# One product of the next pass moved between the last two of a pass, and one quarter of y summed by accumulating DMA

## The chip, the cores and the metric

The kernel runs on one core of a Trainium2 chip, in one launch. The metric is device microseconds (us) of the whole program; three runs were taken, and the median counts. A profiled execution, from which all rows below come, is one further run.

The engines of the core are named as in the profile: PE (TensorE matmul; PEld is its weight load), DVE (VectorE), ACT (ScalarE), POOL (GpSimd) and SP (SyncE). Here POOL and SP mostly issue DMAs. Every engine works through its own list of instructions in order, so an instruction that waits holds up all behind it on that engine.

## The reference, cut to what matters

The layer is a norm, a joint projection, two kinds of attention, an output projection and an MLP with a squared ReLU. The change lies in the last product of the MLP and the sum around it, with 512 tokens, a model width of 2048 and a hidden width of 8192, all float32:

```python
def reference(x, ..., w_up, w_down, norm_final_g):
    ...
    x = x + mix @ w_out[layer]
    u = rmsnorm(x, norm_mlp_g[layer]) @ w_up[layer]
    x = x + jnp.square(jax.nn.relu(u)) @ w_down[layer]
    return rmsnorm(x, norm_final_g)
```

## The kernel before

**Precision.** Each float32 operand is split into a high part, a cast by ACT (`wh` of the weights, `uT` of the activations, line 94), and a low part, a subtraction by DVE (`wl` and the second half of `uT`, line 95). Each product is then three matmuls: high with high, high with low, low with high.

**The down phase** (lines 764 to 845) computes the product of the squared hidden layer with `w_down`. The hidden width is cut into 8 chunks `c` of 1024 rows and the 2048 output columns into 2 halves `n`; a pass is one pair (c, n), 16 in all. Within a pass the 2x2 block product is done by a scheme with 7 block products where 8 would be plain. Each takes sums of blocks of the activations (`o[0]` to `o[6]`, made once per chunk by `chunk_operands`) and sums of blocks of the weights (made in each pass by `down_weights`, a generator that yields the split pairs in the order in which they are used). A product is 24 matmuls of 128x512.

I call the seven products of a pass by the PSUM buffer into which they go: **U1** (`o[0]`), **V** (`o[1]`), **W1** (`o[2]`), **U2** (`o[3]`), **W2** (`o[4]`), **U3** (`o[5]`), **U4** (`o[6]`). Each buffer is two banks. V has its own buffer for each half and is summed over all chunks in PSUM. U1, U2, U3 and U4 add up in one buffer (`pU`) and W1, W2 in another (`pW`). After each of these the running sum is added into a quarter of `y` in SBUF by `to_y`, so U4, which adds to what U3 left, cannot start before `to_y` has read U3's sum. From pass to pass the buffers of U and W change places, since `if n: pU, pW = pW, pU`.

**Who sums y.** In chunks 1 to 6, `to_y` is a DVE add from PSUM (line 800) for W1, U2, W2, U3 and U4. For U1 it is an ACT copy into a tile `st` (line 797) and a DMA from POOL that adds `st` to y (line 798). In chunk 0 the first write of a quarter is an ACT copy into y; in chunk 7 all are DVE adds.

**Weights.** SP loads 512 KB tiles from HBM, and some sums of two blocks come from a second DMA that POOL issues and that adds to the tile in SBUF (line 681). The split pairs `wh`/`wl` have four buffers for the two pairs of each product, so the cast for a product two ahead waits until PE has read a pair of the present one.

The order on the engines is set by a scheduler that works with priorities. The weight work has a high one, and the activation work of the next chunk is pulled ahead into the pass before it. The first matmul of a product is kept in program order.

Of the kernel before, what the change touches and what calls it, by code (L numbers as in the profile page):

```python
# [9 lines left out]
F32 = mybir.dt.float32  # L10
F32R = mybir.dt.float32r
AF = mybir.ActivationFunctionType
ALU = mybir.AluOpType
AX = mybir.AxisListType

P = 128
# [3 lines left out]
NT = SEQ // P  # L20
# [15 lines left out]
def hymba_kernel(ctx: ExitStack, tc: tile.TileContext, x, x_t, norm_mix_g, w_dq, w_dk, w_dv, w_nq, w_nk, w_nv, lams,  # L36
                 subln_g, rel_bias, w_out, norm_mlp_g, w_up, w_down, norm_final_g, cos_t, sin_t, mask_t, out):
    nc = tc.nc
# [546 lines left out]
    for q in range(32):  # L585
# [3 lines left out]
        def prod(ps, s, first, last):  # L589
            th_, tl_ = next(ops)  # L590
            for k in range(8):
                for i, (a, j) in enumerate(((th_, 0), (th_, 1), (tl_, 0))):
                    nc.tensor.matmul(out=ps, lhsT=a[:, k], rhs=s[k // 4][:, j, k % 4], start=first and k + i == 0,  # L593
                                     stop=last and k == 7 and i == 2, skip_group_check=True)
# [26 lines left out]

    up_es.close()
    ps_up.close()
    psD = ctx.enter_context(tc.tile_pool(name="psD", bufs=2, space=bass.MemoryType.PSUM, reuse_waits="tile"))
    ypool = ctx.enter_context(tc.tile_pool(name="ypool", bufs=1, reuse_waits="tile"))
    wd2 = ctx.enter_context(tc.tile_pool(name="wd2", bufs=3, reuse_waits="tile"))
    y = ypool.tile([P, NT, DM], F32, name="y")
# [1 line left out]
    def chunk_operands(c):  # L629

        def load(m, th):
            t = rx.tile([P, 4, 256], F32, name="ur", tag="b")
            nc.sync.dma_start(out=t, in_=ud[4 * c:4 * c + 4, :, (2 * m + th) * 256:(2 * m + th + 1) * 256].rearrange(
                "j p t -> p j t"))
            return t

        pairs = []

        def part(src, neg=False):
            if not pairs or len(pairs[-1]) == 2:  # L640
                pairs.append([])
                pairs[-1].append(tpool.tile([P, 2, 2, 4, 256], F32R, name="uT", tag="T"))
                o = pairs[-1][0][:, 0]
            else:
                o = pairs[-1][0][:, 1]
                pairs[-1].append(None)
            if neg:
                nc.scalar.mul(o[:, 0], src, -1.0)
                nc.vector.scalar_tensor_tensor(out=o[:, 1], in0=src, scalar=-1.0, in1=o[:, 0].bitcast(F32),
                                               op0=ALU.mult, op1=ALU.subtract)  # L650
            else:
                split(o[:, 0], o[:, 1], src)
            return o

        with tc.high_priority(offset=700 if c else 250):
            u11, u12, u21, u22 = load(0, 0), load(1, 0), load(0, 1), load(1, 1)
            o = [part(u11), part(u12)]
            nc.vector.tensor_sub(out=u11, in0=u11, in1=u21)
            nc.vector.tensor_sub(out=u21, in0=u22, in1=u21)
            o.append(part(u21))  # L660
            f = rx.tile([P, 4, 256], F32, name="uf", tag="b")
            nc.vector.tensor_add(out=f, in0=u11, in1=u22)
            o.append(part(f, neg=True))
            nc.vector.tensor_sub(out=f, in0=f, in1=u12)
            o += [part(f), part(u11), part(u22)]
        return o
# [74 lines left out]
    def finish(t, lo, w, col):  # L741
        scaled(t, lo, w)
        squares(t, lo, w, col)
        times_g(t, lo, w)

    def norm_out(t, late=None, cols=3):

        ss = keep.tile([P, 1], F32, name="ssf", tag="ssf", bufs=2)
        nc.vector.tensor_reduce(out=ss, in_=ss3[:, t, :cols], axis=AX.X, op=ALU.add)
        r = rstd_of(keep, ss, DM, 1, "f")  # L750
        for i in ((0, 1, 2, 3) if late is None else (late, 0, 5 - late, 1)):
            qq = slice(i * 512, (i + 1) * 512)
            z = y[:, t, qq]
            if i == late:
                nc.vector.scalar_tensor_tensor(out=z, in0=z, scalar=r, in1=gF[1][:, (i - 2) * 512:(i - 1) * 512],
                                               op0=ALU.mult, op1=ALU.mult)
            elif i >= 2:
                nc.vector.tensor_scalar_mul(z, z, r)
            else:
                nc.scalar.mul(z, z, r)  # L760
            nc.sync.dma_start(out=out[t * P:(t + 1) * P, qq], in_=z)


    pVs = [None, None]
    n_down = [0]
    for c in range(8):
        o = chunk_operands(c)
        for n in range(2):
            end = c == 7 and n == 1
            ops = down_weights(c, n)  # L770
            pU, pW = (psD.tile([P, 2, 512], F32, name="pd", tag="pd") for _ in range(2))
            if n:
                pU, pW = pW, pU
            if c == 0:
                pVs[n] = psD.tile([P, 2, 512], F32, name="pv", tag="pv")
            pV = pVs[n]

            def prod(ps, s, w, first, last=True, blocks=(0, 1)):
                for u in range(2):
                    wh, wl = w[u]  # L780
                    for k in range(2):
                        for b in blocks:
                            sh, sl = (s[:, i, 2 * u + k, b * P:(b + 1) * P] for i in range(2))
                            for i, (l, r) in enumerate(((sh, wh), (sh, wl), (sl, wh))):
                                m = nc.tensor.matmul(out=ps[:, b], lhsT=l, rhs=r[:, k],  # L785
                                                     start=first and u + k + i == 0,
                                                     stop=last and u == 1 and k == 1 and i == 2, skip_group_check=True)
                                if u + k + i == 0:
                                    tc.keep_in_program_order(m)

            def to_y(ps, th, h, neg, fresh=False, dma=False):
                ys = y[:, 2 * th:2 * th + 2, n * 1024 + h * 512:n * 1024 + h * 512 + 512]
                if c == 0 and fresh:
                    nc.scalar.mul(ys, ps, -1.0 if neg else 1.0)
                elif dma:
                    st = wd2.tile([P, 2, 512], F32, name="st", tag="st", bufs=2)
                    nc.scalar.copy(out=st, in_=ps)
                    nc.gpsimd.dma_start(out=ys, in_=st, accum_op=ALU.add)
                else:
                    nc.vector.tensor_tensor(out=ys, in0=ys, in1=ps, op=ALU.subtract if neg else ALU.add)  # L800

            if end:
                for i in range(2):
                    gf = rx.tile([P, 1024], F32, name="gF", tag="b")
                    nc.sync.dma_start(out=gf, in_=norm_final_g[:, i * 1024:(i + 1) * 1024].broadcast_to([P, 1024]))
                    gF.append(gf)
                for t in range(NT):
                    finish(t, 0, 1024, 0)
            prod(pU, o[0], next(ops), True)
            to_y(pU, 0, 0, False, fresh=True, dma=c < 7)  # L810
            prod(pV, o[1], next(ops), c == 0, c == 7)
            if c == 7:
                to_y(pV, 0, 0, False)
            prod(pW, o[2], next(ops), True)
            to_y(pW, 1, 1, True, fresh=True)
            prod(pU, o[3], next(ops), False)
            to_y(pU, 0, 1, True, fresh=True)
            if end:
                for t in (0, 1):
                    finish(t, 1024, 512, 1)  # L820
            prod(pW, o[4], next(ops), False)
            to_y(pW, 0, 1, True)
            if end:
                for t in (0, 1):
                    finish(t, 1536, 512, 2)
                    norm_out(t)
            prod(pU, o[5], next(ops), False)
            to_y(pU, 1, 1, True)
            if not end:
                prod(pU, o[6], next(ops), False)  # L830
                to_y(pU, 1, 0, False, fresh=True)
                continue
            for t in (2, 3):
                finish(t, 1536, 512, 1)
                scaled(t, 1024, 512)
                nc.vector.tensor_add(out=ss3[:, t, 0:1], in0=ss3[:, t, 0:1], in1=ss3[:, t, 1:2])
            w4 = next(ops)
            for b in range(2):
                t = 2 + b
                prod(pU, o[6], w4, False, blocks=(b,))  # L840
                ys = y[:, t, 1024:1536]
                nc.vector.scalar_tensor_tensor(out=ys, in0=pU[:, b], scalar=qs[:, t:t + 1], in1=ys, op0=ALU.mult,
                                               op1=ALU.add)
                squares(t, 1024, 512, 1)
                norm_out(t, late=2, cols=2)


def _shape_tables():
# [82 lines left out]
```

## Time and profile before

| | |
|---|---|
| Median of 3 runs | 2166.03 us (2160.76 to 2166.07) |
| Profiled execution, its own time | 2166.34 us |
| Its span, first to last instruction | 2164.6 us |
| Mean granted TensorE clock | 0.988 of full speed |
| PE busy | 2091.2 us, 97% |
| DVE busy | 1550.5 us, 72% |
| ACT busy | 971.9 us, 45% |
| Down phase | from about 1484 us to the end of the span |

A busy share is an average over stages. PE's figure includes matmuls at a lower clock and the modelled ends of pipelined matmuls. The 1.7 us between the span and the execution's own time lie outside the first and last instruction.

### The profile page before, as it was taken

Reading aid. Unit: us, or ns where it says so; the run is one execution under the profiler, and the core shown is the slowest. Engines: PE = TensorE matmul, PEld = TensorE weight load, DVE = VectorE, ACT = ScalarE, POOL = GpSimd, SP = SyncE. Lnnn points to the kernel's source line nnn. Section 1 sums busy time; section 2 is a strip of 40 time slices with the busy share of each in tenths; the row PEclk is TensorE's granted clock in tenths of the full one; section 3 lists DMA queues with packets and bytes.
Section 4 is the critical chain, followed back from the end, with each engine's and each line's share of the span. In section 5 each row is a group of like instructions: output and inputs, shape, how many; then the busy total and the mean of one; then the engine's idle time right before and its main releaser. Section 6 shows DMA issues by size and latency. Waiting matters only on the chain.

```text
span 2164.6 us, 31127 instructions
## 1 busy us (share of the span) xinstructions
PE 2091.2 (97%) x12604; PEld 1860.7 (86%) x12604; DVE 1550.5 (72%) x1721; ACT 971.9 (45%) x1328; POOL 265.1 (12%) x257
## 2 busy tenths in 40 slices
PE   7999999999999999999999999999999999999986
PEld 6989989989888887999999999998777777777775
DVE  6656556556486437877777877788778778879788
ACT  4444444444354435444443444445544444444444
POOL 4221222122121000000000000000011110111100
PEclk8999999999999999999999999999999999999998
DMA  6332332332233741734334433447767767677663
GB/s 213 119 98 91 97 111 78 103 102 88 93 108 126 255 140 59 237 128 137 129 125 146 139 132 121 147 146 234 193 170 204 195 163 210 182 183 199 179 157 107
DMA packets 105745, 316.18 MB, mean 146 GB/s; under 512 B 11072, under 2 KB 27648, under 8 KB 105600
## 3 DMA queue, kind: packets, MB, share of 16 engines
q1 hardware_dynamic: 83040, 241.33, 33.4%
q0 software_dynamic: 22128, 72.31, 14.4%
q8 instruction: 99, 1.62, 0.3%
q10 hardware_dynamic: 432, 0.53, 0.1%
q14 instruction: 46, 0.38, 0.1%
HBM read 275.33 MB, written 30.25 MB: 141 GB/s over the span
## 4 chain that ended last, share of the span: by engine, by line
PE 85%; DVE 9%; issue 3%; ACT 1%; DMA 1%; SPq 0%; ACTq 0%; DVEq 0%
PE pm L593 27%; PE pd L785 17%; PE pa L141 8%; PE pa L98 7%; PE pa L99 7%; PE pa L100 7%; PE pv L785 4%; DVE wl L95 2%; DVE y L800 2%; PE pb L99 1%; PE pb L98 1%; PE pb L100 1%; PE pc L98 1%; PE pc L99 1%; PE pc L100 1%
## 5 line engine op out<-in xcount | busy, mean ns | idle before, releaser
L94 ACT CAST wh<-b 128x1024 fp32r<-128x1024 f32 x320 | 335.2, 1049 | 511.4 <-PE pd L785 255.6
L785 PE MATMUL pd<-wh,uT 128*128 128x512 f32 x1536 | 490.6, 397 | 36.4 <-DVE y L800 35.2
L95 DVE TENSOR_TENSOR wl<-b,wh 128x1024 fp32r<-128x1024 f32 x320 | 390.7, 1223 | 118.7 <-ACT wh L94 117.4
L785 PEld LDWEIGHTS pd<-wh,uT 128*128 128x128 f32 x1536 | 293.3, 191 | 107.8 <-ACT uT L94 22.0
L785 PE MATMUL pd<-wl,uT 128*128 128x512 f32 x768 | 305.0, 397 | 0.4 <-DVE wl L95 0.3
L593 PE MATMUL pm<-s,wh 128*128 128x256 f32 x1536 | 280.3, 284 | 3.4 <-ACT p L598 2.3
L593 PE MATMUL pm<-a,wh 128*128 128x256 f32 x1536 | 267.4, 279 | 2.0 <-DVE c L611 1.4
L593 PEld LDWEIGHTS pm<-s,wh 128*128 128x128 f32 x1536 | 239.6, 192 | 4.0 <-ACT p L598 2.8
L593 PEld LDWEIGHTS pm<-a,wh 128*128 128x128 f32 x1536 | 232.9, 189 | 2.4 <-DVE c L611 1.6
L95 DVE TENSOR_TENSOR wl<-ts,wh 128x1024 fp32r<-128x1024 f32 x128 | 154.9, 1223 | 105.1 <-ACT wh L94 103.5
L89 ACT CAST wh<-raw 128x1024 fp32r<-128x1024 f32 (+1 forms) x129 | 134.4, 1043 | 199.9 <-PE pa L99 72.1
L593 PE MATMUL pm<-s,wl 128*128 128x256 f32 x768 | 218.3, 284 | 1.5 <-DVE wl L95 1.5
L94 ACT CAST wh<-ts 128x1024 fp32r<-128x1024 f32 x128 | 132.6, 1051 | 186.3 <-PE pm L593 165.2
L141 PE MATMUL pa<-wh,hT 128*128 128x256 f32 x1024 | 201.4, 291 | 14.7 <-DVE hT L166 7.7
L593 PE MATMUL pm<-a,wl 128*128 128x256 f32 x768 | 209.8, 279 | 0.0
L90 DVE TENSOR_TENSOR wl<-raw,wh 128x1024 fp32r<-128x1024 f32 (+1 forms) x98 | 121.0, 1235 | 117.2 <-ACT wh L89 115.9
L100 PE MATMUL pa<-hT,wl 128*128 128x512 f32 x512 | 201.5, 394 | 0.0
L99 PE MATMUL pa<-hT,wh 128*128 128x512 f32 x512 | 201.1, 393 | 0.0
L98 PE MATMUL pa<-hT,wh 128*128 128x512 f32 x512 | 200.9, 392 | 0.0
L141 PEld LDWEIGHTS pa<-wh,hT 128*128 128x128 f32 x1024 | 168.4, 197 | 19.5 <-DVE hT L166 9.2
L785 PEld LDWEIGHTS pd<-wl,uT 128*128 128x128 f32 x768 | 146.9, 191 | 32.8 <-DVE wl L95 1.2
L593 PEld LDWEIGHTS pm<-s,wl 128*128 128x128 f32 x768 | 147.4, 192 | 1.9 <-DVE wl L95 1.9
(250 smaller groups left out, 3565.7 us busy)
## 6 DMA issues: line engine op xcount, KB each, us to landing
b<-in_w_down SPq DMA_DIRECT2D x130, 512.0 KB, 4.1
b<-in_w_up SPq DMA_DIRECT2D x128, 512.0 KB, 3.7
b<-in_w_down POOLq DMA_DIRECT2D x64, 512.0 KB, 9.1
raw<-in_w_out SPq DMA_DIRECT2D x32, 512.0 KB, 3.4
ud<-c POOLq DMA_DIRECT2D x32, 512.0 KB, 3.2
ur<-ud SPq DMA_DIRECT2D x32, 512.0 KB, 10.2
raw<-in_w_dq SPq DMA_DIRECT2D x16, 512.0 KB, 3.3
raw<-in_w_dk SPq DMA_DIRECT2D x16, 512.0 KB, 3.3
```

Of the source, the lines that this page charges most:

```text
L89: nc.scalar.copy(out=wh[:, cs], in_=raw[:, cs])
L90: eng.tensor_sub(out=wl[:, cs], in0=raw[:, cs], in1=wh[:, cs].bitcast(F32))
L94: nc.scalar.copy(out=hi, in_=src)
L95: (eng or nc.vector).tensor_sub(out=lo, in0=src, in1=hi.bitcast(F32))
L98: nc.tensor.matmul(out=ps, lhsT=lh, rhs=rh, start=first, stop=False)
L99: nc.tensor.matmul(out=ps, lhsT=lh, rhs=rl, start=False, stop=False)
L100: nc.tensor.matmul(out=ps, lhsT=ll, rhs=rh, start=False, stop=last)
L141: nc.tensor.matmul(out=ps[t], lhsT=a, rhs=b[:, k, :], start=first and i == 0, stop=last and i == 2, skip_group_check=True)
L593: nc.tensor.matmul(out=ps, lhsT=a[:, k], rhs=s[k // 4][:, j, k % 4], start=first and k + i == 0, stop=last and k == 7 and i == 2, skip_gro ...
L785: m = nc.tensor.matmul(out=ps[:, b], lhsT=l, rhs=r[:, k], start=first and u + k + i == 0, stop=last and u == 1 and k == 1 and i == 2, skip ...
L800: nc.vector.tensor_tensor(out=ys, in0=ys, in1=ps, op=ALU.subtract if neg else ALU.add)
```

## The change

Two buffers `X[0]` and `X[1]` (two banks each) take the place of the rotating `pU`/`pW`: pass p uses `X[p % 2]` as pU and the other as pW. The first product of pass p+1, with its weights and, at a new chunk, with its activation operands, is issued by `start_pass(p + 1)` between U3 and U4 of pass p. It goes into the buffer that was pW. The sum of the first quarter from U1 is now a DVE add. The quarter that W1 and U3 feed is now summed by ACT copies (with the sign) and accumulating DMAs from POOL in chunks 0 to 6, except for the first write of chunk 0.

```diff
-            prod(pU, o[0], next(ops), True)
-            to_y(pU, 0, 0, False, fresh=True, dma=c < 7)
...
-            prod(pW, o[2], next(ops), True)
-            to_y(pW, 1, 1, True, fresh=True)
...
-            prod(pU, o[5], next(ops), False)
-            to_y(pU, 1, 1, True)
-            if not end:
-                prod(pU, o[6], next(ops), False)
-                to_y(pU, 1, 0, False, fresh=True)
-                continue
+    X = [psD.tile([P, 2, 512], F32, name=f"x{i}") for i in range(2)]
+    V = [psD.tile([P, 2, 512], F32, name=f"v{i}") for i in range(2)]
...
+        elif dma:
+            st = wd2.tile([P, 2, 512], F32, name="st", tag="st", bufs=2)
+            nc.scalar.mul(st, ps, -1.0 if neg else 1.0)
+            nc.gpsimd.dma_start(out=ys, in_=st, accum_op=ALU.add)
...
+    def start_pass(p):
+
+        c, n = divmod(p, 2)
+        if n == 0:
+            chunks[c] = chunk_operands(c)
+        ops = down_weights(c, n)
+        prod(X[p % 2], chunks[c][0], next(ops), True)
+        to_y(c, n, X[p % 2], 0, 0, False, fresh=True)
+        return ops
...
+        pU, pW = X[p % 2], X[1 - p % 2]
...
+        prod(pW, o[2], next(ops), True)
+        to_y(c, n, pW, 1, 1, True, fresh=True, dma=c < 7)
...
+        prod(pU, o[5], next(ops), False)
+        to_y(c, n, pU, 1, 1, True, dma=c < 7)
+        if not end:
+            ops_n = start_pass(p + 1)
+            prod(pU, o[6], next(ops), False)
+            to_y(c, n, pU, 1, 0, False, fresh=True)
+            ops = ops_n
+            continue
```

**On ACT**, at the end of the second pass of chunk 1, before. The two `wh` casts from `b_15480` and `b_15482` are the weights of U4, those from `b_15769` and `b_15771` of the next pass's U1, and `uT` are operands of chunk 2:

```order
L94 CAST wh_15703<-b_15480 128x1024
L94 CAST wh_15707<-b_15482 128x1024
L94 CAST wh_15773<-b_15769 128x1024
L94 CAST wh_15777<-b_15771 128x1024
L94 CAST uT_15759<-ur_15736 128x1024
L94 CAST uT_15759<-uf_15754 128x1024
```

The same place on ACT now; `b_15734` and `b_15736` are the next U1's weights, `b_15445` and `b_15447` those of U4, and `st_15700` is the copy of U3's sum:

```order
L94 CAST wh_15738<-b_15734 128x1024
L94 CAST wh_15742<-b_15736 128x1024
L94 CAST wh_15773<-b_15445 128x1024
L94 CAST wh_15777<-b_15447 128x1024
L94 CAST uT_15726<-ur_15703 128x1024
L787 ACTIVATE st_15700<-x1_14641 128x1024
L94 CAST uT_15726<-uf_15721 128x1024
```

The weights of U4 and of the next U1 have changed places, and the copy of U3's sum stands behind one operand cast.

**On DVE**, at the same place, before; the two adds to y are those of W2 (`pd_15478`) and U3 (`pd_15479`):

```order
L95 TENSOR_TENSOR wl_15704<-b_15480,wh_15703 128x1024
L800 TENSOR_TENSOR y_14638<-y_14638,pd_15478 128x2x512
L95 TENSOR_TENSOR wl_15708<-b_15482,wh_15707 128x1024
L664 TENSOR_TENSOR uf_15754<-uf_15754,ur_15738 128x1024
L95 TENSOR_TENSOR wl_15774<-b_15769,wh_15773 128x1024
L800 TENSOR_TENSOR y_14638<-y_14638,pd_15479 128x2x512
```

And now; the adds are those of W2 (the first, from `x0`), of the next U1 (the second, from `x0`) and of U4 (from `x1`):

```order
L95 TENSOR_TENSOR wl_15739<-b_15734,wh_15738 128x1024
L790 TENSOR_TENSOR y_14638<-y_14638,x0_14640 128x2x512
L95 TENSOR_TENSOR wl_15743<-b_15736,wh_15742 128x1024
L664 TENSOR_TENSOR uf_15721<-uf_15721,ur_15705 128x1024
L95 TENSOR_TENSOR wl_15774<-b_15445,wh_15773 128x1024
L95 TENSOR_TENSOR wl_15778<-b_15447,wh_15777 128x1024
L95 TENSOR_TENSOR uT_15726<-ur_15703,uT_15726 128x1024
L95 TENSOR_TENSOR uT_15726<-uf_15721,uT_15726 128x1024
L95 TENSOR_TENSOR wl_15813<-b_15808,wh_15812 128x1024
L790 TENSOR_TENSOR y_14638<-y_14638,x0_14640 128x2x512
L95 TENSOR_TENSOR wl_15817<-b_15810,wh_15816 128x1024
L95 TENSOR_TENSOR wl_15845<-b_15734,wh_15844 128x1024
```

The add for U3 is gone from DVE, and the add for U4 follows the last row shown.

**On POOL**, over the same pass, before; `b` are accumulating weight loads, those of `b_15769` and `b_15771` for the next pass's W1:

```order
L681 DMA b_15954<-in_w_down 128x1024
L681 DMA b_16209<-in_w_down 128x1024
L681 DMA b_15769<-in_w_down 128x1024
L681 DMA b_15771<-in_w_down 128x1024
L798 DMA y_14638<-st_15805 128x2x512
```

And now; `st_15587` is W1's copy, `st_15700` U3's, `st_15876` the next pass's W1's, and `b_15734`, `b_15736` are the loads for the next W1:

```order
L788 DMA y_14638<-st_15587 128x2x512
L681 DMA b_15954<-in_w_down 128x1024
L681 DMA b_16209<-in_w_down 128x1024
L681 DMA b_15734<-in_w_down 128x1024
L681 DMA b_15736<-in_w_down 128x1024
L788 DMA y_14638<-st_15700 128x2x512
L788 DMA y_14638<-st_15876 128x2x512
```

Each pass now has two DMAs into y on this queue, both behind the weight loads of the pass end. Over the whole program there are 26 of them, where there were 12.

## Rows read from the trace of the kernel before

**Rows 1.** The page: busy time by engine, and the last chain by line.

```profile
PE 2091.2 (97%) x12604; PEld 1860.7 (86%) x12604; DVE 1550.5 (72%) x1721; ACT 971.9 (45%) x1328; POOL 265.1 (12%) x257
...
PE pm L593 27%; PE pd L785 17%; PE pa L141 8%; PE pa L98 7%; PE pa L99 7%; PE pa L100 7%; PE pv L785 4%; DVE wl L95 2%; DVE y L800 2%; PE pb L99 1%; PE pb L98 1%; PE pb L100 1%; PE pc L98 1%; PE pc L99 1%; PE pc L100 1%
```

**Rows 2.** Waits of line 785, down phase: releaser, us in total, times.

```profile
  DVE y L800: 35.2, 16
```

**Rows 3.** Timeline of PE: matmuls behind a wait; idle before in brackets.

```profile
1558.61 0.47 PE L785 MATMUL pd<-wh,uT 128*128 128x512 f32 x1 [1.41 <-DVE y L800]
...
1640.68 0.47 PE L785 MATMUL pd<-wh,uT 128*128 128x512 f32 x1 [3.27 <-DVE y L800]
...
2101.29 0.47 PE L785 MATMUL pd<-wh,uT 128*128 128x512 f32 x1 [2.81 <-DVE y L800]
...
2143.68 0.47 PE L785 MATMUL pd<-wh,uT 128*128 128x512 f32 x1 [1.52 <-DVE y L800]
```

**Rows 4.** Chain that ended last, down phase: start us, us, what.

```profile
1495.19 21.98 PE pd L785 x96
...
1518.56 11.23 PE pd L785 x48
1529.79 5.46 PE pv L785 x24
...
1640.68 12.84 PE pd L785 x48
...
1724.32 13.99 PE pd L785 x48
```

**Rows 5.** Busy us by stretch: PE, PEld, DVE, ACT, POOL; clock, DMA share, GB/s.

```profile
1300.00:1400.00 100.00, 100.00 (x856) 100.00 (x855) 77.39 (x78) 42.60 (x56) 2.66 (x5) 1.00 0.41 138
...
1558.60:1598.80 40.20, 38.78 (x169) 31.50 (x169) 29.95 (x26) 19.05 (x19) 4.65 (x5) 1.00 0.80 209
1598.80:1640.60 41.80, 38.62 (x168) 31.39 (x168) 35.86 (x32) 21.11 (x21) 4.63 (x5) 1.00 0.66 176
1640.70:1682.40 41.70, 40.30 (x168) 32.57 (x169) 31.10 (x27) 16.54 (x16) 4.67 (x5) 0.96 0.77 199
...
1724.40:1767.20 42.80, 41.40 (x169) 33.41 (x169) 31.04 (x27) 16.54 (x16) 4.68 (x5) 0.93 0.75 196
...
1976.20:2017.80 41.60, 40.20 (x168) 32.53 (x168) 31.11 (x27) 16.55 (x16) 4.65 (x5) 0.96 0.76 199
```

**Rows 6.** Timeline of DVE, last two passes: start, us, what, idle before.

```profile
2099.93 1.22 DVE L800 TENSOR_TENSOR y<-y,pd 128x1024 f32<-128x1024 f32 x1
...
2107.03 1.23 DVE L95 TENSOR_TENSOR wl<-b,wh 128x1024 fp32r<-128x1024 f32 x1 [3.62 <-ACT wh L94]
...
2142.31 1.23 DVE L800 TENSOR_TENSOR y<-y,pd 128x1024 f32<-128x1024 f32 x1
```

**Rows 7.** Timeline of ACT around a copy of `st`.

```profile
1653.55 1.05 ACT L94 CAST wh<-b 128x1024 fp32r<-128x1024 f32 x1 [1.67 <-PE pd L785]
1654.51 1.00 ACT L797 COPY st<-pd 128x1024 f32<-128x1024 f32 x1
```

**Rows 8.** All that writes or reads `st`: duration ns min/median/max, first and last start.

```profile
L797 ACT COPY st<-pd x12: 1003/1005/1011, 1571.3 to 2030.1; 128x1024 f32<-128x1024 f32 x12
L798 POOL DMA_DIRECT2D y<-st x12: 1187/1200/1218, 1572.6 to 2031.5; - x12
...
DMA to landing us min/median/max: 5.0/5.0/6.8
```

**Rows 9.** DMA, 1640 to 2060 us: queues (packets, MB, share of 16 engines), issues.

```profile
q1 hardware_dynamic: 21329, 52.49, 37.9%
q0 software_dynamic: 8507, 26.31, 33.8%
...
b<-in_w_down POOLq DMA_DIRECT2D x41, 512.0 KB, 9.1
ur<-ud SPq DMA_DIRECT2D x17, 512.0 KB, 10.7
```

More of the change, by code (lines that the diff above doesn't have):

```diff
@@ L623, in hymba_kernel @@
     ps_up.close()
-    psD = ctx.enter_context(tc.tile_pool(name="psD", bufs=2, space=bass.MemoryType.PSUM, reuse_waits="tile"))
+    psD = ctx.enter_context(tc.tile_pool(name="psD", bufs=1, space=bass.MemoryType.PSUM, reuse_waits="tile"))
     ypool = ctx.enter_context(tc.tile_pool(name="ypool", bufs=1, reuse_waits="tile"))
@@ L761, in norm_out @@
             nc.sync.dma_start(out=out[t * P:(t + 1) * P, qq], in_=z)
-    pVs = [None, None]
     n_down = [0]
[L766 to L808, printed above, removed]
-            prod(pU, o[0], next(ops), True)
-            to_y(pU, 0, 0, False, fresh=True, dma=c < 7)
-            prod(pV, o[1], next(ops), c == 0, c == 7)
-            if c == 7:
-                to_y(pV, 0, 0, False)
-            prod(pW, o[2], next(ops), True)
-            to_y(pW, 1, 1, True, fresh=True)
[L816 to L826, printed above, removed]
-            prod(pU, o[5], next(ops), False)
-            to_y(pU, 1, 1, True)
-            if not end:
-                prod(pU, o[6], next(ops), False)
-                to_y(pU, 1, 0, False, fresh=True)
-                continue
[L833 to L845, printed above, removed]
@@ new lines, in hymba_kernel, with prod @@
+    X = [psD.tile([P, 2, 512], F32, name=f"x{i}") for i in range(2)]
+    V = [psD.tile([P, 2, 512], F32, name=f"v{i}") for i in range(2)]
+    def prod(ps, s, w, first, last=True, blocks=(0, 1)):
+        for u in range(2):
+            wh, wl = w[u]
+            for k in range(2):
+                for b in blocks:
+                    sh, sl = (s[:, i, 2 * u + k, b * P:(b + 1) * P] for i in range(2))
+                    for i, (l, r) in enumerate(((sh, wh), (sh, wl), (sl, wh))):
+                        m = nc.tensor.matmul(out=ps[:, b], lhsT=l, rhs=r[:, k], start=first and u + k + i == 0,
+                                             stop=last and u == 1 and k == 1 and i == 2, skip_group_check=True)
+                        if u + k + i == 0:
+                            tc.keep_in_program_order(m)
@@ new lines, in to_y @@
+    def to_y(c, n, ps, th, h, neg, fresh=False, dma=False):
+        ys = y[:, 2 * th:2 * th + 2, n * 1024 + h * 512:n * 1024 + h * 512 + 512]
+        if c == 0 and fresh:
+            nc.scalar.mul(ys, ps, -1.0 if neg else 1.0)
+        elif dma:
+            st = wd2.tile([P, 2, 512], F32, name="st", tag="st", bufs=2)
+            nc.scalar.mul(st, ps, -1.0 if neg else 1.0)
+            nc.gpsimd.dma_start(out=ys, in_=st, accum_op=ALU.add)
+        else:
+            nc.vector.tensor_tensor(out=ys, in0=ys, in1=ps, op=ALU.subtract if neg else ALU.add)
@@ new lines, in hymba_kernel @@
+    chunks = {}
+    def start_pass(p):
[6 more added lines that the diff above has]
+        return ops
+    ops = start_pass(0)
+    for p in range(16):
+        c, n = divmod(p, 2)
+        o = chunks[c]
+        pU, pW = X[p % 2], X[1 - p % 2]
+        end = p == 15
+        if end:
+            for i in range(2):
+                gf = rx.tile([P, 1024], F32, name="gF", tag="b")
+                nc.sync.dma_start(out=gf, in_=norm_final_g[:, i * 1024:(i + 1) * 1024].broadcast_to([P, 1024]))
+                gF.append(gf)
+            for t in range(NT):
+                finish(t, 0, 1024, 0)
+        prod(V[n], o[1], next(ops), c == 0, c == 7)
+        if c == 7:
+            to_y(c, n, V[n], 0, 0, False)
+        prod(pW, o[2], next(ops), True)
+        to_y(c, n, pW, 1, 1, True, fresh=True, dma=c < 7)
+        prod(pU, o[3], next(ops), False)
+        to_y(c, n, pU, 0, 1, True, fresh=True)
+        if end:
+            for t in (0, 1):
+                finish(t, 1024, 512, 1)
+        prod(pW, o[4], next(ops), False)
+        to_y(c, n, pW, 0, 1, True)
+        if end:
+            for t in (0, 1):
+                finish(t, 1536, 512, 2)
+                norm_out(t)
+        prod(pU, o[5], next(ops), False)
[6 more added lines that the diff above has]
+            continue
+        for t in (2, 3):
+            finish(t, 1536, 512, 1)
+            scaled(t, 1024, 512)
+            nc.vector.tensor_add(out=ss3[:, t, 0:1], in0=ss3[:, t, 0:1], in1=ss3[:, t, 1:2])
+        w4 = next(ops)
+        for b in range(2):
+            t = 2 + b
+            prod(pU, o[6], w4, False, blocks=(b,))
+            ys = y[:, t, 1024:1536]
+            nc.vector.scalar_tensor_tensor(out=ys, in0=pU[:, b], scalar=qs[:, t:t + 1], in1=ys, op0=ALU.mult,
+                                           op1=ALU.add)
+            squares(t, 1024, 512, 1)
+            norm_out(t, late=2, cols=2)
```

## The prediction

> **What bounds the kernel now.** I read the page first: PE is busy 97% of the span, and the chain that ended last runs mostly through matmuls, with the adds to y (line 800) among the few other entries [rows 1]. The reader is to see that only PE's gaps and PE's speed can be gained, and that line 800 is where DVE enters the chain.
>
> Next come the waits of the down phase. PE sat idle 35.2 us before line 785 until an add to y was done, 16 times [rows 2]. PE's timeline shows where: once per pass, at the first matmul of U4. In the three passes up to the first of chunk 1, and in the first passes of chunks 2 to 6, the gap is 1.41 us: one DVE add and its start. In the second passes of chunks 1 to 6 it is 3.27 us, since DVE there also makes the next chunk's operands and comes late to the add. The first pass of chunk 7 has 2.81 us, and the last pass, which ends otherwise, 1.52 us [rows 3]. 8 x 1.41 + 6 x 3.27 + 2.81 + 1.52 is 35.2, so nothing is left over.
>
> Then the table by pass. A pass holds 38.6 us of PE work at full clock (the stretch from 1598.8 us). The passes after a 3.27 us gap show a granted clock of 0.93 to 0.96 and 40.2 to 41.4 us of PE busy time [rows 5]: part of the pass ran at the lower of the two levels, 1.2 instead of 2.4 GHz, after PE had stood still. Five of the six such passes lost 1.5 to 2.8 us each, together 9.1 us; the sixth lost nothing.
>
> **Removed: the wait before U4.** With the next U1 between U3 and U4, whoever reads U3's sum has a whole product of time, 5.46 us [rows 4]. If nothing else stops PE, products follow each other at 5.46 us. From the end of the first U3 (1495.19 + 21.98 = 1517.2) to the end of U3 in the fifteenth pass (2101.29 - 2.81 = 2098.5) [rows 3, 4] are 581.3 us for 14 passes of 7 products. At 5.46 us these 98 products take 535.1 us, so 46.2 us go. The parts agree: 14 waits are 35.2 - 2.81 - 1.52 = 30.9 us, the lower clock 9.1 us, and 6.2 us are left, 0.44 per restart. A pair of products after a wait takes 11.23 us where two take 10.92 [rows 4], and the last matmul's modelled end is counted before a wait but not in running work. The sure part is 30.9 + 9.1 = 40.0 us, the upper end 46.2. I take 46.2, since running products are seen at 5.46 us and PE stayed at a clock of 1.00 over 100 us without a gap [rows 5].
>
> **Moved: who reads U3's sum.** It is ACT now. At a chunk's end its list after U3 is: second cast for U4 (1.05 us, starts about 0.1 after U3's end, when its buffer is free), an operand cast (about 1.05), the copy (1.00) [rows 7, 8]. That is 3.2 us after U3, and U4 starts 5.46 after it, so 2.3 us are spare. At the end of a first pass no operand cast stands there, and 3.3 us are spare. W1's copy similarly ends 2.2 us after W1, and W2 needs the buffer 5.46 after W1. The cost on PE is nothing as long as ACT is not 2.3 us later than this.
>
> **DVE.** It loses two adds per pass and gets one back (U1's). In a second pass it had 35.86 us of work in 41.8 us [rows 5], 32 operations. With 31 it has about 34.7 us, in a pass of 38.2. I followed its new list at one operation per 1.14 us (1.22 us each, a little overlapped), each no earlier than its cast or product. W2's add starts 1.8 us after W2 and ends 2.6 before the next U1 wants that buffer. The next U1's low parts are ready 3.7 us before their use. U4's add ends 1.6 us after U4, where the next W1 comes 5.46 after it. So DVE costs nothing, but in the second passes it is 91% full.
>
> **Added: 14 more DMAs into y.** Each is a POOL issue of 1.20 us that waits for its ACT copy and lands 5.0 us later [rows 8]. The next copy into the same `st` tile comes a pass later, so that is hidden. What waits behind it on POOL are accumulating weight loads for a later U3. The loads for the next W1 stand ahead of U3's DMA: they issue about 1 us after U3's end, land after 9.1 us [rows 9], and their cast is due some 11 us after U3's end at the earliest and 18 at the latest. On the 16 DMA engines the software queue took 33.8% of 420 us for 26.31 MB [rows 9], so a 0.52 MB DMA takes 2.8 us of them. A pass has taken (0.379 + 0.338) x 41.7 = 29.9 us; with one more it is 32.7 of 38.2 us, 86%. The stretch from 1558.6 us had 80% in 40.2 us [rows 5] without a wait for weights. The bounds are nothing and the rival on DMA below; I take nothing, as in that row.
>
> The Trainium skill (DMA: Bandwidth & Descriptors, "Issuing engines are not separate DMA queues") says that DMAs issued by SP and GpSimd run on the same 16 engines and interleave. By that rule the extra y traffic slows the weight loads too, and the sum would move towards the rival on DMA; the landing of 10.7 us for `ur` beside 5.0 us for y [rows 8, 9] does not decide it.
>
> **The last pass.** Its end is not rearranged. From the add for U3 of the fifteenth pass to that for U3 of the sixteenth DVE needs 2142.31 + 1.23 - 2099.93 - 3.62 = 40.0 us of nearly unbroken work [rows 6], and its list still holds the same operations. PE needs 7 x 5.46 = 38.2. So DVE bounds the last pass, and the last U4 starts about 1.5 + 40.0 + 0.1 = 41.7 us after the fifteenth U3, against 2143.68 - 2098.48 = 45.2 [rows 3]: 3.5 us gained, behind a wait of about 3 us that stays. After waits of 3.27 us the next 48 matmuls took up to 13.99 instead of 11.23 us [rows 4], so the last product may lose 0 to 2.8 us; I take 0.5, since it is 24 matmuls and one of six such waits cost nothing.
>
> The Trainium skill (TensorE: Matmul & The Clock Gate, "What's actually happening") has the half rate follow idleness as a rule. By it the last product would lose more of the 2.8 us, and the sum would be up to 2.3 us higher, inside the range below; no row shows this place with so long a wait.
>
> **Sum.** 46.2 + 3.5 - 0.5 = 49.2 us. The profiled execution took 2166.3 us, 0.3 above the median of the runs. 2166.3 - 49.2 gives 2117 us.
>
> **The rivals.**
>
> *Half the gain.* The second passes keep a stall. DVE is 91% full there, and if its list slips by 3 us, the next U1 waits for W2's add in the shared buffer, as U4 did for U3's. Then only the eight waits of 1.41 us with 0.44 each (14.8 us) and the end (3 us) go: 2148 us. For it speaks that DVE was late in just these passes; against it the 2.6 us spare and the operation fewer.
>
> *DMA becomes the bound (slower).* At 86% the accumulating loads for W1 land later. Up to a landing of about 17 us nothing happens; beyond it each us is a us per pass in 14 passes. Doubled to 18.2 us it costs 1 to 2 us per pass, 2130 to 2145 us; from about 20.5 us (3.5 us per pass, 49 us) on the kernel is no faster, and at 22 us it takes 2187. For it speak the 10.7 us of `ur`, against it the stretch at 80%.
>
> *The change doesn't do it.* U4 waits for ACT instead of DVE, because the copy stands behind casts that wait for PE. If ACT is 4 us later than worked out, 1.7 us return per pass with the restart cost: 14 x (1.7 + 0.44) = 30 us, so 2147 us without loss of clock, and with all of the 9.1 us back 2156. The order of the list speaks against it.
>
> **How the numbers follow.** I give the forecast 0.70 (2111 to 2125, from the spread of the runs before and the clock at the end), half the gain 0.12, DMA 0.11 (0.04 of it mild, 0.07 at or past the old time), U4 waiting for ACT 0.05, and something too small to measure 0.02. 0.3% of this kernel is 6.5 us, about what a measurement can tell from no change, so faster means below 2159.5. That gives 0.89 faster, 0.04 same and 0.07 slower. For 8 in 10 the range reaches from 2110 to half the gain, 2148.
>
> **What would show it.** Right: PE without a wait on line 800's successor except in the last pass; passes of 38.2 to 38.6 us at a clock of 1.00; the U3 copy on ACT about 3.2 us after U3. Wrong: idle PE behind W2's add (half the gain), behind `wh` casts that wait for a DMA (DMA), or behind `st` copies (ACT). The forecast fails if PE waits more than about 1 us per pass for anything.

## The result, and the profile after

The changed kernel takes 2128.2 us (median of 4 runs, 2122.47 to 2129.51) against 2165.7 us (4 runs, 2160.76 to 2166.07): a ratio of 0.983, with a 95% interval of 0.980 to 0.985. It is faster, inside the range of 2110 to 2148, and 11 us above the 2117 that were forecast. The profiled execution took 2128.14 us with a span of 2126.0; the numbers below come from it.

The page, busy time by engine and the last chain by line, to be held against [rows 1]:

```profile
PE 2080.7 (98%) x12604; PEld 1853.7 (87%) x12604; DVE 1527.0 (72%) x1707; ACT 982.5 (46%) x1342; POOL 282.6 (13%) x271
...
PE pm L593 28%; PE x L776 13%; PE pa L141 8%; PE pa L98 7%; PE pa L99 7%; PE pa L100 7%; DMA b<-in_w_down 5%; DVE wl L95 3%; PE v L776 2%; PE pb L99 1%; PE pb L98 1%; PE pb L100 1%; DVE b L685 1%; PE pc L98 1%; PE pc L99 1%
```

The adds to y (now line 790) have left the list, and weight loads that were not in it (`b<-in_w_down`) now hold 5% of the chain. The reader is to see that the old wait is gone and that the chain now passes through DMAs, which had 1% of it before.

The waits of the matmuls (line 776), down phase: releaser, us in total, times. They answer to [rows 2].

```profile
  DVE y L790: 7.8, 7
  issue: 4.5, 6
  ACT wh L94: 4.0, 3
  ACT junk L735: 3.2, 1
  DVE wl L95: 3.0, 5
  DVE y L850: 2.1, 2
```

35.2 us in 16 waits on DVE's add have become 7.8 in 7. The view counts the idle time of PE's weight loads together with that of its matmuls. The waits for `wh` are all of weight loads, and the kernel before had more of them (14.5 us in 8). Of the matmuls alone, two waited for `wl`, 0.16 and 0.70 us. The table by pass, of four passes, answers to [rows 5].

```profile
1603.90:1642.40 38.50, 38.50 (x170) 31.57 (x170) 35.44 (x31) 20.87 (x21) 5.89 (x6) 1.00 0.77 202
1642.40:1682.10 39.70, 38.68 (x170) 31.41 (x169) 26.82 (x23) 17.58 (x18) 5.92 (x6) 1.00 0.81 210
1682.10:1722.00 39.90, 38.92 (x170) 31.38 (x169) 36.77 (x32) 21.30 (x22) 5.87 (x6) 1.00 0.82 203
1722.00:1760.40 38.40, 38.40 (x169) 31.46 (x168) 28.39 (x25) 18.24 (x18) 5.91 (x6) 1.00 0.88 235
```

The granted clock is 1.00, and PE is busy for the whole of the first and the last of these passes. From one V to the next, ten of the fifteen passes take 38.40 to 38.46 us, and five take 39.71, 39.88, 40.65, 39.36 and 40.19. These five hold 7.7 us more than undisturbed ones would.

How the first of them comes about is seen around 1631 us, the end of a U3. First the timeline of POOL:

```profile
1630.63 0.89 POOL L681 DMA_DIRECT2D b<-in_w_down  x1 [11.96 <-DMA b<-in_w_down]
1631.95 2.60 POOL L681 DMA_DIRECT2D b<-in_w_down  x3 [0.43 <-issue]
1634.80 1.20 POOL L788 DMA_DIRECT2D y<-st  x1 [0.25 <-ACT st L787]
```

Then ACT:

```profile
1633.49 1.02 ACT L787 ACTIVATE st<-x 128x1024 f32<-128x1024 f32 x1
...
1645.49 1.05 ACT L94 CAST wh<-b 128x1024 fp32r<-128x1024 f32 x1 [7.29 <-DMA b<-in_w_down]
```

DVE:

```profile
1646.57 1.22 DVE L95 TENSOR_TENSOR wl<-b,wh 128x1024 fp32r<-128x1024 f32 x1 [6.47 <-ACT wh L94]
1647.71 1.21 DVE L790 TENSOR_TENSOR y<-y,x 128x1024 f32<-128x1024 f32 x1
```

And PE, with the gap that follows, and the one before the last U4, which answers to the last of [rows 3]:

```profile
1649.07 0.47 PE L776 MATMUL x<-wh,uT 128*128 128x512 f32 x1 [1.02 <-DVE y L790]
...
2104.20 0.47 PE L776 MATMUL x<-wh,uT 128*128 128x512 f32 x1 [2.83 <-DVE y L790]
```

The four accumulating weight loads (two for the next W1, two for a later U3) were issued one behind the other. In the chain the load that mattered took 12.89 us from 1632.50, where [rows 9] had a median of 9.1. ACT's cast waited 7.29 us for it and DVE's low split 6.47 for the cast. U4's add into y stands behind that split in DVE's queue. V ended at about 1648.0, but W1 needs the bank that U4's add reads, so PE stood still for 1.02 us. So a late load reaches PE by way of an add that has nothing to do with it.

Three of the five passes, all of them second passes (39.88, 40.65 and 39.36 us), take another way. There PE stands still at U3, which adds to what U2 left, until DVE's add of U2 is done. Two of these gaps on PE:

```profile
1705.18 0.47 PE L776 MATMUL x<-wh,uT 128*128 128x512 f32 x1 [0.98 <-DVE y L790]
...
1861.20 0.47 PE L776 MATMUL x<-wh,uT 128*128 128x512 f32 x1 [1.29 <-DVE y L790]
```

What came before the first of them, from the chain, from ACT and from DVE:

```profile
1672.08 14.41 DMA b<-in_w_down
```

```profile
1686.59 2.00 ACT L94 CAST wh<-b 128x1024 fp32r<-128x1024 f32 x2 [3.93 <-DMA b<-in_w_down]
```

```profile
1703.83 1.21 DVE L790 TENSOR_TENSOR y<-y,x 128x1024 f32<-128x1024 f32 x1
```

Early in the pass, ACT's cast waited 3.93 us for a load that took 14.41. DVE then works without a pause from the split that follows this cast (1687.67) to U2's add (1703.83), and the add ends too late. The list of a second pass is so full that DVE cannot make up the lost time before U3. In the fifth pass (40.19 us, between the last two) PE waits 0.51 us at W1 and 0.70 within U2 for a split.

The DMA view of 1640 to 2060 us, to be held against [rows 9] (queue: packets, MB, share of 16 engines; issue: count, KB, median us to landing):

```profile
q0 software_dynamic: 11817, 33.20, 42.9%
q1 hardware_dynamic: 21858, 55.79, 38.9%
...
b<-in_w_down SPq DMA_DIRECT2D x82, 512.0 KB, 6.6
b<-in_w_down POOLq DMA_DIRECT2D x43, 512.0 KB, 10.4
y<-st POOLq DMA_DIRECT2D x20, 512.0 KB, 11.9
```

### The profile page after: what moved, and what is told of

Same layout as the page of the kernel before. It is cut to its first block, busy times and chain, and to the rows that moved or that the text cites. A ratio compares the mean times of both kernels' runs of the same rounds, so it can differ in the third digit from the quotient of the medians.

```text
span 2126.0 us, 31142 instructions
## 1 busy us (share of the span) xinstructions
PE 2080.7 (98%) x12604; PEld 1853.7 (87%) x12604; DVE 1527.0 (72%) x1707; ACT 982.5 (46%) x1342; POOL 282.6 (13%) x271
## 4 chain that ended last, share of the span: by engine, by line
PE 81%; DVE 8%; DMA 5%; issue 2%; ACT 2%; POOL 0%; SPq 0%; ACTq 0%; DVEq 0%; POOLq 0%
PE pm L593 28%; PE x L776 13%; PE pa L141 8%; PE pa L98 7%; PE pa L99 7%; PE pa L100 7%; DMA b<-in_w_down 5%; DVE wl L95 3%; PE v L776 2%; PE pb L99 1%; PE pb L98 1%; PE pb L100 1%; DVE b L685 1%; PE pc L98 1%; PE pc L99 1%
## 5 line engine op out<-in xcount | busy, mean ns | idle before, releaser
L776 PE MATMUL x<-wh,uT 128*128 128x512 f32 x1536 | 482.0, 392 | 8.7 <-DVE y L790 7.8
L776 PEld LDWEIGHTS x<-wh,uT 128*128 128x128 f32 x1536 | 288.8, 188 | 76.5 <-issue 4.5
L776 PE MATMUL x<-wl,uT 128*128 128x512 f32 x768 | 301.2, 392 | 0.9 <-DVE wl L95 0.9
L776 PEld LDWEIGHTS x<-wl,uT 128*128 128x128 f32 x768 | 144.5, 188 | 33.1 <-DVE wl L95 2.2
```

What stands on the lines that cost most here:

```text
L776: m = nc.tensor.matmul(out=ps[:, b], lhsT=l, rhs=r[:, k], start=first and u + k + i == 0, stop=last and u == 1 and k == 1 and i == 2, skip ...
```

## The experiments

Theory A: the gain comes from the new order of products alone. Theory D: the y DMAs cost what is missing to the forecast. The rivals were that DVE's relief brings the gain (B), that DVE's own order makes the waits (E), and that POOL's order does (F). Three chips were used: one for the new order alone, the changed sums alone, no accumulating DMA and W1's loads first; a second for the narrow DMAs, three y DMAs, all sums on DVE and the multiplications on GpSimd; a third for the last three. Each ratio is to the kernel before on the same chip. Theory G, in the last runs, says that the last pass is bound by DVE.

**The new order alone.** To the changed kernel:

```
 start_pass: to_y(..., X[p % 2], 0, 0, False, fresh=True, dma=c < 7)
 W1 and U3:  to_y(...)            # without dma=c < 7
```

> The new order of products alone: the sums into y are shared out as in the kernel before (U1 by an ACT copy and an accumulating DMA, W1 and U3 by DVE). Theory A (the gain comes from putting the next pass's U1 between U3 and U4; the changed sums only make room on DVE): nearly the whole gain stays, 2118 to 2132 us, and U4 no longer waits 2.2 us in each pass for DVE's add of U3, as that add has U1's 5.46 us to lie behind. Theory B (DVE, 91% busy in a second pass, needs the relief by the copies, or its backlog reaches the products): 2138 to 2150 us, with waits of products on DVE of 1.5 us or more in each pass. One accumulating DMA of y a pass in place of two also means that, if these DMAs make the weight loads late (theory D below), the loads of W1 land nearer to the 9.1 us of before than to 13.

2121.26 us (5 runs), ratio 0.980 (0.978 to 0.982). All passes from V to V take 38.40 or 38.46 us, but for one of 39.87 between the last two. No add of U3 is waited for in them. A holds and B is out: DVE carries one add more than in the changed kernel and is busier, and no product waits for it, but for 1.07 us in that one pass. Two passes of this run by stretch, columns as in [rows 5]:

```profile
1647.10:1685.50 38.40, 38.40 (x170) 31.51 (x169) 29.77 (x26) 15.60 (x16) 4.71 (x5) 1.00 0.78 201
1685.50:1723.90 38.40, 38.40 (x169) 31.48 (x168) 36.28 (x33) 22.04 (x22) 4.63 (x5) 1.00 0.82 217
```

The loads for W1 and U3 landed after 9.7 us here, between 9.1 and 10.4.

**The changed sums alone.** To the kernel before:

```
 U1:        to_y(pU, 0, 0, False, fresh=True)          # was dma=c < 7
 W1 and U3: to_y(..., True, dma=c < 7), copied with nc.scalar.mul(st, ps, -1.0)
```

> The kernel before with only the sums into y shared out as in the changed kernel (W1 and U3 by an ACT copy and an accumulating DMA, U1 by DVE); the order of products is the old one. Theory A: U4 still stands directly behind U3 on the same banks, so it waits for the copy instead of the add: at least 1.0 us a pass for the copy itself, against 2.2 us now, so that at most 14 x 1.2 = 17 us are gained: 2148 to 2166 us. Theory B (the relief of DVE brings the gain): 2125 to 2142 us. A third way (ACT's copy queues behind casts and more DMA traffic delays weights): above 2168 us.

2176.4 us (6 runs), ratio 1.005 (1.003 to 1.007): slower than before, past the interval of A. B falls. The third way comes nearest in time, though for its first half alone, as two timelines show, PE's and ACT's:

```profile
1649.59 0.50 PE L785 MATMUL pd<-wh,uT 128*128 128x512 f32 x1 [3.00 <-ACT st L797]
```

```profile
1647.57 1.04 ACT L94 CAST uT<-ur 128x1024 fp32r<-128x1024 f32 x1
1648.52 1.02 ACT L797 ACTIVATE st<-pd 128x1024 f32<-128x1024 f32 x1
```

Right behind U3, U4 waits for the copy, and the copy stands behind casts in ACT's queue. Here it is 3.00 us, where DVE's add had 3.27 [rows 3]; in the first passes it is 2.06, where the add had 1.41. Over the 14 passes with a copy the waits are 36.4 us, where the add had 30.9. The copy is no shorter way out of the bank; a product in between hides it.

**No accumulating DMA into y.** The line `nc.gpsimd.dma_start(out=ys, in_=st, accum_op=ALU.add)` is left out.

> The changed kernel without the accumulating DMAs into y; the ACT copies of W1 and U3 stay, and their two products of each pass are left out of the sum in y. Theory D (the waits left over in five passes of the changed kernel, 7.8 us in all, come from weight loads that land 11 to 15 us after issue because the accumulating DMAs of y, 7.3 MB and two a pass, share the DMA engines): the loads of W1's weights land within 10 us, the waits nearly go, 2117 to 2122 us. Theory E (they come from DVE's own order: U4's add and a low split that stand behind one another) or theory F (the accumulating loads are issued late, behind those of t3 on POOL's queue): 2125 to 2129 us, with the same waits at W1 and V.

2120.81 us (4 runs), ratio 0.979 (0.978 to 0.981). All fifteen passes take 38.40 or 38.46 us, the loads land after a median of 8.6 us, and POOL still issues the four weight loads together at each pass end. DVE's work is the same too, so E and F are out as sole causes.

**The same DMAs, narrow.** It tells their bytes from their place in POOL's queue:

```
-nc.gpsimd.dma_start(out=ys, in_=st, accum_op=ALU.add)
+nc.gpsimd.dma_start(out=ys[:, :, :32], in_=st[:, :, :32], accum_op=ALU.add)
```

> The changed kernel with its accumulating DMAs into y narrowed from 512 to 32 columns per row, in the same places on POOL's queue; the other 480 columns of these two products are left out of the sum in y. Theory D in the form that their bytes count: 2118 to 2123 us, the accumulating weight loads land after a median of 8.6 us as without them. Theory D in the form that their place on POOL's queue or their number of descriptors counts: 2125 to 2130 us, landing as in the changed kernel.

2120.0 us (4 runs), ratio 0.979 (0.978 to 0.981), again without a disturbed pass. The DMA view of 1640 to 2060 us, and the split and add of DVE in the pass shown above:

```profile
b<-in_w_down SPq DMA_DIRECT2D x82, 512.0 KB, 4.6
b<-in_w_down POOLq DMA_DIRECT2D x43, 512.0 KB, 9.4
...
y<-st POOLq DMA_DIRECT2D x20, 32.0 KB, 7.5
```

```profile
1643.91 1.22 DVE L95 TENSOR_TENSOR wl<-b,wh 128x1024 fp32r<-128x1024 f32 x1 [3.64 <-ACT wh L94]
1645.05 1.21 DVE L790 TENSOR_TENSOR y<-y,x 128x1024 f32<-128x1024 f32 x1
```

The same chain runs 2.7 us earlier (1643.91 for 1646.57), and the add is done before W1 wants its bank. Their bytes count; their number, and their place in this queue, cost nothing that shows once the bytes are few. The median landing of POOL's loads fell only to 9.4 us, not to the 8.6 expected. The median says little (with all sums on DVE, a run below without any DMA into y, it is 9.7): over 1500 to 2060 us ACT's casts waited for weights 77.5 us in the changed kernel, 32.1 in this run and 27.5 without the DMAs.

**Three y DMAs a pass.** The changed kernel with `dma=c < 7` for U1 too.

> The changed kernel with U1's sum by ACT copy and accumulating DMA as well: three such DMAs a pass, 0.5 MB each, where the changed kernel has two and the run with the new order alone one. Theory D (these DMAs make the accumulating weight loads late): disturbed passes in more than five of the sixteen, 2134 to 2160 us. If they cost by chance of place and not by their number: 2125 to 2131 us. If ACT or DVE relief counted: below 2124 us.

2131.86 us (4 runs), ratio 0.985 (0.983 to 0.986). Seven passes take 39.18 to 40.86 us. The time is below the 2134 expected: the third DMA costs less than the second. In the DMA view of the same window:

```profile
q0 software_dynamic: 14573, 38.59, 49.6%
...
b<-in_w_down SPq DMA_DIRECT2D x82, 512.0 KB, 7.1
b<-in_w_down POOLq DMA_DIRECT2D x40, 512.0 KB, 10.3
```

**All sums on DVE.** `dma=False` for W1 and U3.

> The new order of products with all six sums of a pass on DVE: no ACT copy and no accumulating DMA into y after the first two passes. DVE's work in a second pass grows from 36.3 us in the run with the new order alone to some 37.5 of 38.4 us. Theory A with D (the order gives the gain, the y DMAs cost): 2117 to 2123 us, no disturbed pass, and also the one late load of that run's pass 14 goes. The rival that DVE's backlog eats half of the gain: waits on DVE of 1 us or more in most second passes, 2128 to 2148 us.

2120.44 us (4 runs), ratio 0.979 (0.978 to 0.981). DVE at 36.49 us of a pass of 38.40 (1608.1 to 1646.5 us; 37.5 were expected) delays nothing where the loads are on time. The late load in pass 14, which was to go, stayed: the pass between the last two takes 40.18 us, and a load of 15.46 us stands in its chain. So relief by ACT was not needed at all. The runs in one table, first V to last V, from PE's timeline:

| y DMAs of 0.5 MB a pass | run | 15 passes, us | longer than 39 us | median time, us |
|---|---|---|---|---|
| 0 | narrow DMAs | 576.48 | 0 | 2120.0 |
| 0 | left out | 576.48 | 0 | 2120.81 |
| 0 | all sums on DVE | 578.20 | 1 | 2120.44 |
| 1 | new order alone | 577.89 | 1 | 2121.26 |
| 2 | changed kernel | 584.19 | 5 | 2128.2 |
| 3 | three DMAs | 586.73 | 7 | 2131.86 |

The passes are those of one profiled execution of each run. The pass between the last two is long with no y DMA (all sums on DVE), with one, two and three, and short only in the two runs that keep ACT's copies but not the bytes. What makes it long is open. Without it the other fourteen passes go with the y DMAs: none is long up to one DMA a pass, four are with two, and six with three. Five of these six wait at U3 for U2's add, as above. The y DMAs are not the only source of late loads, though: in the last run below, again with all sums on DVE, the pass before that one takes 39.54 us, behind a load of 14.59. By the medians the cost of two y DMAs is less sharp: the interval of the changed kernel (0.980 to 0.985) touches those of the runs with none or one (up to 0.981 and 0.982), and one of its four executions took 2122.47 us. With three DMAs the interval lies clear of those with none.

**W1's loads first on POOL.** The accumulating loads are kept in program order, with U3's (t3) loads moved behind W1's:

```
             for u in range(2):
                 plus(ch[u], u, 1)
+            t3 = [load(wd2, "t3", u, 3, 1) for u in range(2)]
 plus:       m = nc.gpsimd.dma_start(...);  tc.keep_in_program_order(m)
```

> The changed kernel with POOL's queue in another order: the two accumulating loads for W1's weights stand ahead of the two for U3's weights (t3) of the same pass, where they stood behind t3 loads of a later pass that wait for their first halves to land. Theory F (the order on POOL's queue makes W1's weights late): the loads are issued up to 2 us earlier and the waits of W1 on DVE and ACT go, 2117 to 2123 us. Theory D (the traffic of the y DMAs makes them late whatever the order): 2125 to 2129 us. A loss is possible too: U3's weights now come later, two products ahead of their use, and if they land after 15 us or more U3 waits for its split: 2130 us or more.

2161.25 us (12 runs), ratio 0.998 (0.997 to 0.999). The order put more behind than was meant: the four loads now also stand behind U3's y DMA, which waits for ACT's copy, as POOL's timeline shows:

```profile
1646.75 1.19 POOL L790 DMA_DIRECT2D y<-st  x1 [16.59 <-ACT st L789]
1647.48 4.00 POOL L681 DMA_DIRECT2D b<-in_w_down  x4
```

POOL's loads now take 13.8 us (median), and fourteen of fifteen passes take 39.90 to 45.16 us. PE's matmuls and weight loads together wait 28.7 us for `wh` and 26.0 for `wl` (the matmuls alone 7.9 and 8.6). The run does not test F as intended. Nearly the whole gain goes when POOL's loads are issued in this order, behind the y DMA. How much of that is the place of the y DMA, and how much the moved loads of U3, was not separated.

**The last pass: multiplications on GpSimd.** To the new order alone:

```
-        nc.vector.tensor_mul(out=y[:, t, lo:lo + w], ...)
+        (nc.gpsimd if w == 1024 else nc.vector).tensor_mul(out=y[:, t, lo:lo + w], ...)
```

> The new order alone, and of the last pass's finishing work the four multiplications of the first half of y by the gain (128x1024, 1.15 us each on DVE) on GpSimd, which does no other arithmetic there. Theory G (the last pass is bound by DVE, 38.0 us busy of 39.3): its waits on DVE, 3.5 us, shrink by 2 to 3.5 us, 2117 to 2120 us. Rival (something else ends the wait, or the GpSimd multiplications, 2.6 us each by the row of that shape, slow DVE down): no change, 2120 to 2124 us, or slower.

2123.16 us (5 runs), ratio 0.981 (0.979 to 0.982); without the edit 0.980 (0.978 to 0.982). The rival holds. POOL's timeline, then DVE's:

```profile
2073.64 7.81 POOL L739 TENSOR_TENSOR y<-y,gF 128x1024 f32<-128x1024 f32 x2 [10.47 <-ACT junk L735]
```

```profile
2058.62 5.63 DVE L95 TENSOR_TENSOR wl<-b,wh 128x1024 fp32r<-128x1024 f32 x2
...
2079.12 3.42 DVE L685 TENSOR_TENSOR b<-b 128x1024 f32<-128x1024 f32 x1
```

**The last pass: adds by DMA.** To the new order alone, for U4's weights (the first run: the last pass; the second: the last two; the third: the last pass, on the kernel with all sums on DVE):

```
         for u in range(2):
-            add(ch[u], b21[u])
+            plus(ch[u], u, 2) if c + n == 8 else add(ch[u], b21[u])
```

> The new order alone, and in the last pass the second half of U4's weights is added by two accumulating DMAs from DRAM (0.5 MB each) in place of two adds on DVE (1.13 us each). In that stretch DVE is busy 38.0 of 39.3 us and the DMA engines 16% of the time. Theory G (the last pass is bound by DVE): 2.3 us of DVE's work less shortens its waits of 3.5 us by 1 to 2.3 us: 2118.5 to 2120.5 us. Rival (the wait is set by the order of single steps, not by DVE's amount of work, or the two loads land late, as they are issued behind U2's split): 2121 us or more, with a wait on ACT's cast or a DMA ahead of U4.

> The same in the last two passes. The pass before the last has all its sums on DVE too and is 1.4 us longer than the others in the run with the new order alone (39.87 against 38.46 us). If that is DVE's amount of work: another 1 to 1.4 us less, 2117 to 2119.5 us. If it comes from loads that land late there (DMA 57% busy): no change against the last pass alone, or up to 2 us more.

> All six sums on DVE, and U4's weights of the last pass by accumulating DMAs as in the first run of this call. Theory G: 1 to 2.3 us less than with all sums on DVE alone (2120.4 us): 2118 to 2119.5 us. Rival: 2120 us or more.

2118.55 us (4 runs), ratio 0.979 (0.977 to 0.980); 2117.94 us (5 runs), 0.978 (0.977 to 0.979); and 2118.09 us (4 runs), 0.978 (0.977 to 0.980). The wait ahead of the last U4 fell, as PE's timelines of the new order alone and of the first of these runs show:

```profile
2097.09 0.76 PE L776 MATMUL x<-wh,uT 128*128 128x512 f32 x1 [2.82 <-DVE y L790]
```

```profile
2096.49 0.47 PE L779 MATMUL x<-wh,uT 128*128 128x512 f32 x1 [1.51 <-DVE y L793]
```

From the last V to the last U4 PE takes 29.09 us in the first two runs and 29.10 in the third, where it took 31.36 with the new order alone and with all sums on DVE. These 2.3 us are what the two adds take on DVE (1.13 us each), so the last pass is bound by DVE's amount of work. In the time of the whole program the gain is not clear by itself: the intervals overlap those without the edit (0.978 to 0.982 and 0.978 to 0.981). The two loads landed after 5.4 us. In the second run the wait between the last two passes stays (1.04 us, for `wl`, beside 1.07), and its interval overlaps the first run's: it is not DVE's amount of work. The late load named in the expectation fits (the chain with the new order alone has one of 15.10 us from 2015.07), but was not tested by itself. Each of the three has a ratio below those of both kernels.

## Why the prediction was right, and where it was off

The kernel is faster and the time lies in the stated range. It does not lie in the narrower 2111 to 2125 us that had a chance of 0.70: 2128.2 is just past it, close to the mild form of the rival on DMA (from 2130).

**The wait before U4: right.** All 14 waits are gone, and every one of the fifteen passes shows a granted clock of 1.00, so the 9.1 us of the clock came back with the waits. From the second V to the last, 14 passes of 7 products, the 535.1 us forecast are 545.7 in the changed kernel and 538.0 with the narrow DMAs. The 2.9 us between 538.0 and 535.1 are the pace: running products follow each other at 38.43 / 7 = 5.49 us, and 5.46 was the length of one group of the chain [rows 4]. So of the 6.2 us put down to restarts only 3.3 came back.

**ACT's copy: right.** It ended at 1634.51, about 3.1 us after U3's end, against 3.2 forecast, and nothing waits for it. The run with the changed sums alone shows the price where no product covers it.

**DVE: right as long as the loads are on time.** Then it delays nothing even with all six sums. But "DVE costs nothing" left out what a late load does to a list that is 91% full. "U4's add ends 1.6 us after U4" left out that the split of W1's weights stands ahead of the add in DVE's queue, and that it waits for a load. U2's add, for which U3 waits, was not worked out at all, and there PE stood still for 0.98, 1.29 and 0.46 us in three second passes. That is the reason of the rival "half the gain", a list that slips, at another add and a smaller size, and a late load set it off. A queue with the adds ahead of the splits would test this by itself; it was not tried.

**Added DMAs: the failed term.** "I take nothing" was worth up to 7.7 us in the profile, 6.0 without the pass between the last two, which is as long with no y DMA. The step that failed is the threshold: "up to a landing of about 17 us nothing happens". It counted from the load to its own product, but the loads reach PE earlier through the adds of U4 and U2, and 12.89 and 14.41 us were enough. The mild form of the rival on DMA is what happened, at a smaller price than its 2130 to 2145 us, since five of fifteen passes were hit, by 1.0 to 2.2 us each. The row taken as evidence, a stretch at a DMA share of 0.80 without a wait, was true and no proof: undisturbed passes here have shares of 0.77 and 0.88, disturbed ones 0.81 and 0.82. The share doesn't tell; when the loads of one burst land, and how much spare time DVE has behind them, does.

On this the rule cited from the Trainium skill (DMA: Bandwidth & Descriptors, "Issuing engines are not separate DMA queues") pointed the right way. The traces agree: plain weight loads on SP's queue landed after 4.6 us with narrow DMAs on POOL, after 6.6 with two full ones a pass and after 7.1 with three. With one full one a pass (the new order alone) it was 4.4, no later than with none (4.5 and 4.6).

**The last pass: right in kind.** From the fifteenth U3's end at about 2061.9 to the last U4 at 2104.20 are 42.3 us, forecast 41.7, behind a wait of 2.83 us, forecast about 3. From there to the end of the span are 21.8 us where [rows 3] leave 20.9: 0.9 lost, forecast 0.5. The first half of the last U4 ran partly at the lower clock: 0.64 of full speed was granted in the 4.7 us after its wait, 1.00 in the 42.2 before.

**Sum.** 7.7 (late loads) + 2.9 (pace) + 0.6 (last pass) + 0.4 (its end) is 11.6 us over the forecast; a start of the down phase about 1 us earlier takes some back, and 11 were measured.

## What to carry to other kernels

When a copy or an add stands between two products on one bank, put another product between them before moving the add to another engine: here the order alone gave the gain, and the engine change alone lost. When a transfer is added, follow the late load through every queue in which something stands behind it, not only to the instruction that uses the data, and ask how much spare time the engine behind it has: DVE at 36 of 38.4 us delayed nothing until a load came late. An average DMA share did not tell the disturbed passes from the others; adding a third transfer, narrowing it and leaving it out did.

## What the runs showed that was not expected

The size of what GpSimd does to DVE was not expected. A multiplication of 128x1024 on GpSimd beside a busy DVE took 3.3 to 3.9 us, where other arithmetic of this shape had taken 2.4 to 2.7 there and DVE needs 1.14 from start to start. DVE's own instructions stretched meanwhile: two splits took 5.63 us instead of 2.35, a third 2.30 instead of 1.22, an add 3.42 instead of 1.22. That is 6.6 us lost on DVE for 4.6 saved. The Trainium skill (GPSIMD Engine Reference, "8. Key points") says that the two share their SBUF interfaces and contend when DVE reads two SBUF inputs; the run agrees for these four instructions, which read two such inputs, though another split in that time (at 2074.63) kept its 1.22 us. The sums from PSUM beside them kept their 1.20 and 1.21 us.
